# Sink column, merged weight sums, and value halves added in DRAM, in a one-core hybrid decoder layer

## Chip, cores and metric

The kernel runs on one core of a Trainium2 chip. The metric is the device time of one execution in microseconds; three timed runs of the kernel before gave 1900.37, 1901.0 and 1901.44 us, the median being 1901.0.

## What is computed

One layer of a hybrid decoder on x of 2048 tokens and 1024 channels, all in float32. After an RMS norm one input projection gives nine column groups. Branch A is a gated causal convolution of width 3. Branch B is sliding-window attention (window 128, 16 query heads, 4 key heads of 64, a norm on queries and keys, and a learned sink for every query head). Both branches are gated, projected, merged by sigmoid gates and projected once more.

```python
q = rms_norm(q.reshape(b, s, N_Q_HEADS, HEAD_DIM), q_norm_g)
k = rms_norm(k.reshape(b, s, N_KV_HEADS, HEAD_DIM), k_norm_g)
...
scores = einsum(qb, kb) * HEAD_DIM ** -0.5       # blocks of 128 queries, 256 keys
scores = where(valid, scores, NEG_INF)           # 0 <= q_pos - k_pos < 128
m = maximum(max(scores), sink)
p = exp(scores - m)
p = p / (sum(p) + exp(sink - m))
o = einsum(p, vb) * silu(z_a)
...
merged = g_a * (y_c @ w_conv_out) + g_b * (o @ w_attn_out)
return x + merged @ w_out
```

## The kernel before

**Tiles and products.** The sequence is cut into two tiles of 1024 tokens, which run one after the other. The projections are computed by a Strassen-like scheme: a unit of 256 output columns takes seven products (X, V, Y and so on) in place of eight, each product being twelve matmuls of 512 columns (`product`, L634: four chunks, and for each one high x high, high x low and low x high parts of the float32 numbers). Such a scheme needs sums of weight blocks and of input blocks. The sums of the weights are formed by VectorE in `sums` inside `pieces_of` (L516): one addition and three subtractions of 128x512 for a unit (two of the 81 units form them in another order, L528 and L535). ScalarE and VectorE then split each block into its high and low part.

**The clock of the program.** All order is written out by hand: `manual_schedule` keeps the order of issue on every engine. `run` (L889) advances a counter, the tick, with each product, and after each product issues what `put` has filed under that tick: pieces of weight preparation, evacuations and attention steps. Each engine has one queue and takes its instructions in that order; ScalarE, SyncE and GpSimd also issue transfers (SyncE most of them). `vec` (L284) weaves waiting VectorE steps in between others.

**Attention.** There are 64 blocks, 32 for each tile: 4 key heads by 8 blocks of 128 queries. `attention` (L1865) gives block r a tick n from the lists STEPS_0 and STEPS_1, three to nine ticks apart, and files its steps relative to n:

- n-5: loads of queries and keys (SyncE); n+4: load of values.
- n: `att_scores` (L1227). TensorE writes scores of both halves of the block and four heads into one score bank `s` (`sp`, one buffer): for each half one matmul of 384 columns (low parts of the keys), then two of 192 columns. VectorE copies the masked part over, takes the maximum (128 columns for each head), multiplies it with the query norm `rq`, takes the minimum with the negated sink, and adds the sink: five small results in `st`.
- n+1: `att_exp` (L1260). ScalarE takes the exponential of the sink term, and of the four heads with their sums.
- n+2: `att_norm` (L1270) adds the sink term, takes the reciprocal and scales; `att_flip` transposes 32x32 blocks on VectorE, and GpSimd stores the result `fd`; n+4: GpSimd loads it back transposed in four transfers.
- n+9 and n+10: ScalarE and VectorE form high and low parts (`xh`, `xl`); GpSimd masks them with four selects (`att_low`, L1303).
- n+13: `att_values` (L1324): six matmuls of 256 columns into a bank `po`.
- n+14: `att_out` (L1335). In `po` the partitions 0 to 63 and 64 to 127 hold two partial sums of the same result. ScalarE copies, crosswise, the other half of the partitions into `o`, with two copies of 64x256.
- n+15: `att_sum` (L1346). VectorE adds the own halves with two additions of 64x256, and SyncE stores `o` (128 KB) to `od` in DRAM.

The gate `za` loads `od` later (`fin_z`, L1422), in the order of the key heads, and multiplies it. Of the buffers, `big` has 19 slots of 2 KB a partition, which nearly all of the above share; `small` has 12 for each kind of small result.

Of the kernel before, what the change touches and what calls it, by code (L numbers as in the profile page):

```python
# [83 lines left out]
SUM_WAIT = 5  # L84
VALUES_LATER = ((0, 10), (0, 30))
# [40 lines left out]
def block_kernel(  # L126
# [23 lines left out]
    small = ctx.enter_context(tc.tile_pool(name="small", bufs=12))  # L150
# [68 lines left out]
    nsink_r = consts.tile([P, NKV, 2, 2], F32, name="nsink_r")  # L219
# [8 lines left out]
    def prep_cols():  # L228
# [5 lines left out]
        nc.vector.tensor_scalar(  # L234
            out=nsink_r, in0=sink_r, scalar1=-1.0, scalar2=None, op0=ALU.mult)
# [224 lines left out]
    def pieces_of(n):  # L460
# [37 lines left out]
        if kind in "SP":  # L498
# [509 lines left out]
    rqs = {}  # L1008
# [14 lines left out]
    def fin_q(t, j):  # L1023
# [58 lines left out]
        def by_query(r):  # L1082

            rq = consts.tile([P, 2, HB, 2, 2], F32, tag="rq", bufs=4, name=f"rq{t}_{j}")
            if not by_pe:
                vec.tensor_copy(rq, r.rearrange("p (c q b h) -> p q b h c", c=2, q=2, h=2))
                rqs[t, j] = rq
# [5 lines left out]
            rqs[t, j] = rq  # L1093
# [133 lines left out]
    def att_scores(t, j, b, ld):  # L1227
# [4 lines left out]
        sp = ps_s.tile([P, 2, 2, 2 * P], F32, tag="s", name=f"s{nm}")  # L1232
        for h in range(2):
            skip = (2 - h) * HD if first else 0
            keys = slice(h * HD + skip, (h + 3) * HD)
            nc.tensor.matmul(
                sp[:, h, :, skip : 3 * HD], lhsT=kq[:, 1, h * P : (h + 1) * P], rhs=kz[:, :, keys],
                start=True, stop=False)
            for c in range(2):
                nc.tensor.matmul(  # L1240
                    sp[:, h, c, skip : 3 * HD], lhsT=q2[:, h, c, :], rhs=kq[:, 0, keys],
                    start=False, stop=c == 1)
# [10 lines left out]
        mul(st[:, 5].rearrange("p (h c) -> p h c", c=2), st[:, 0].rearrange("p (h c) -> p h c", c=2), rv)  # L1253
        vec.scalar_tensor_tensor(
            out=st[:, 1], in0=st[:, 5], scalar=-1.0, in1=nsink_r[:, j].rearrange("p h c -> p (h c)"),
            op0=ALU.mult, op1=ALU.min)
        add(st[:, 2], sink_r[:, j].rearrange("p h c -> p (h c)"), st[:, 1])
        return sg, st, rv

    def att_exp(t, j, b, got):  # L1260
        sg, st, rv = got
        nc.scalar.activation(out=st[:, 3], in_=st[:, 2], func=AF.Exp)
        p = slot([P, G, P], F32, f"p{t}_{j}_{b}")
        for i in range(G):
            nc.scalar.activation(  # L1265
                out=p[:, i, :], in_=sg[:, i, HD : 3 * HD], func=AF.Exp, bias=st[:, 1, i : i + 1],
# [79 lines left out]
    def att_sum(t, j, b, got):  # L1346
        o, parts = got
        for ov, pv in parts:
            add(ov, pv, ov)
# [789 lines left out]
```

## Time and profile before

| what | value |
|---|---|
| median of three runs | 1901.0 us |
| profiled execution, its own time | 1900.13 us |
| its span, first to last instruction | 1898.4 us |
| TensorE matmul rows busy | 1888.9 us |
| VectorE busy | 1547.3 us |
| ScalarE busy | 986.6 us |
| GpSimd busy | 590.5 us |
| moved by DMA | 402.22 MB |

In the profile PE is TensorE's matmuls, PEld its weight loads, DVE VectorE, ACT ScalarE, POOL GpSimd and SP SyncE. Times are in microseconds, those of single instructions in nanoseconds. A group's row gives line, engine, operation, result and operands by the program's names, shapes, count, then busy time and mean; behind the second bar stands the idle time of the engine just before, and what ended it. A row of waits gives who waited for whom, the sum, how often, and the longest. Line 278 is that of a helper through which most VectorE steps go, so these are told apart by tile names. Matmuls overlap, so their durations are longer than the distance from one start to the next; the distance is what counts. Granted clock 1.00 is TensorE at full clock.

### The profile page before, as it was taken

To read this page: it belongs to the slowest core of one execution; us is meant where nothing else is said; L and a number is where in the kernel's file an instruction comes from. 1 tells how busy PE (TensorE), PEld (TensorE's weight loads), DVE (VectorE), ACT (ScalarE), POOL (GpSimd) and SP (SyncE) were. 2 spreads that over 40 slices of the span, in tenths; PEclk is the share of its full clock that TensorE was granted. 3 is DMA by queue.
4 is the path that set the end of the run, shared out by engine and by line. 5 is a ranking of instruction groups with operands and counts; after the bars stand their busy time and mean duration, and the time that the engine had idled before them with its cause. 6 is when DMAs were issued, how large, how long until landed. Compare 5 with 4: busy or idle time off the path is not lost.

```text
span 1898.4 us, 27426 instructions
## 1 busy us (share of the span) xinstructions
PE 1888.9 (100%) x8670; PEld 1572.3 (83%) x8670; DVE 1547.3 (82%) x2620; ACT 986.6 (52%) x1967; POOL 590.5 (31%) x846
## 2 busy tenths in 40 slices
PE   9999999999999999999999999999999999999999
PEld 7888888888888888888888888888888888888887
DVE  7988898898888767669799899888888777787754
ACT  7665455456666443434565545556666434444321
POOL 2073335335655000011462344445556000121000
PEclk9999999999999999999999999999999999999999
DMA  8286555558777857894584655567788887779653
GB/s 294 80 239 178 166 159 171 172 183 248 240 237 230 301 195 247 281 279 113 170 229 118 193 165 152 168 200 234 235 247 270 300 280 267 274 193 269 212 176 111
DMA packets 222497, 402.22 MB, mean 212 GB/s; under 512 B 30032, under 2 KB 104784, under 8 KB 212880
## 3 DMA queue, kind: packets, MB, share of 16 engines
q1 hardware_dynamic: 188224, 313.10, 50.4%
q0 software_dynamic: 30528, 78.94, 16.0%
q10 hardware_dynamic: 3600, 8.42, 1.3%
q8 instruction: 69, 1.13, 0.2%
q14 instruction: 76, 0.62, 0.1%
HBM read 271.09 MB, written 129.25 MB: 211 GB/s over the span
## 4 chain that ended last, share of the span: by engine, by line
PE 89%; DVE 5%; DMA 2%; ACT 2%; issue 1%; SPq 0%; POOL 0%; DVEq 0%; ACTq 0%; POOLq 0%
PE Y L640 33%; PE Xcv L640 4%; PE Vcv L640 4%; PE ya L1468 4%; PE Vq L640 2%; PE Xq L640 2%; PE Xyb L640 2%; PE Vyb L640 2%; PE Vo L640 2%; PE Xo L640 2%; PE Vza L640 2%; PE Xza L640 2%; PE po L1330 2%; PE Xgb L640 2%; PE Vgb L640 2%; PE Xga L640 2%
## 5 line engine op out<-in xcount | busy, mean ns | idle before, releaser
L1292 POOL DMA_DIRECT2D x<-fd x256 | 139.6, 552 | 128.8 <-DMA fd<-f 55.6
L1265 ACT ACTIVATE p<-s,st,rq 128x128 f32<-128x128 f32 x256 | 113.0, 450 | 0.1
L1313 POOL TENSOR_SCALAR_AFFINE_SELECT xh<-xh 64x512 fp32r<-64x512 f32 x64 | 59.3, 927 | 152.7 <-DVE xl L278 103.7
L1285 POOL DMA_DIRECT2D fd<-f x64 | 36.9, 577 | 209.4 <-DVE f L278 173.4
L1551 POOL DMA_DIRECT2D mt<-tha x16 | 13.8, 862 | 255.0 <-DVE tha L278 233.4
L640 PE MATMUL Xcv<-oph,wcv_ah 128*128 128x512 f32 x256 | 79.2, 390 | 0.0
L1313 POOL TENSOR_SCALAR_AFFINE_SELECT xl<-xl 64x512 fp32r<-64x512 f32 x64 | 66.2, 1034 | 4.4
L1313 POOL TENSOR_SCALAR_AFFINE_SELECT yp<-xl 64x512 fp32r<-64x512 f32 x64 | 58.2, 909 | 3.1
L1313 POOL TENSOR_SCALAR_AFFINE_SELECT yp<-yp 64x512 fp32r<-64x512 f32 x64 | 57.4, 898 | 4.2
L278 DVE SCALAR_TENSOR_TENSOR y<-u,cols,y 128x512 f32<-128x512 f32 x64 | 53.3, 834 | 3.8 <-ACT y L1379 2.7
L278 DVE TENSOR_TENSOR o<-po,o 64x256 f32<-64x256 f32 x128 | 53.4, 417 | 2.7 <-ACT o L1342 1.7
L640 PEld LDWEIGHTS Xcv<-oph,wcv_ah 128*128 128x128 f32 x256 | 47.6, 188 | 9.6
L278 DVE TENSOR_TENSOR p<-p,st 128x512 f32<-128x512 f32 x64 | 50.5, 790 | 3.3
L469 ACT CAST wcv_sh<-wcv_raw 128x1024 fp32r<-128x1024 f32 x16 | 16.8, 1051 | 69.7 <-DVE wcv_raw L278 69.7
L1265 ACT ACTIVATION_READ_ACCUMULATOR p<-s,st,rq 128x1 f32 x256 | 50.7, 198 | 0.0
L1342 ACT COPY o<-po 64x256 f32<-64x256 f32 x128 | 47.1, 368 | 6.2 <-DMA wpd_yb<-wph_yb 3.0
L1070 POOL DMA_DIRECT2D q2d<-q_h x64 | 44.2, 690 | 18.1 <-ACT q_h L1065 9.2
L640 PE MATMUL Xcv<-oph,wcv_al 128*128 128x512 f32 x128 | 49.8, 389 | 0.0
L2040 POOL DMA_DIRECT2D oc<-ocd x12 | 6.5, 543 | 136.0 <-DMA wyb_sh<-wpd_yb 119.7
L1070 POOL DMA_DIRECT2D q2d<-q_l x64 | 44.1, 689 | 13.7 <-DMA q2d<-q_h 5.0
L278 DVE TENSOR_TENSOR wcv_raw<-wcv_raw 128x512 f32<-128x512 f32 x64 | 47.3, 758 | 1.1
L278 DVE STREAM_TRANSPOSE f<-p 128x512 f32<-128x512 f32 x64 | 45.5, 711 | 2.9 <-DVE p L278 0.2
(713 smaller groups left out, 6457.9 us busy)
## 6 DMA issues: line engine op xcount, KB each, us to landing
gd<-th SPq DMA_DIRECT2D x64, 256.0 KB, 2.7
wcv_raw<-in_w_units SPq DMA_DIRECT2D x16, 1024.0 KB, 5.4
q<-q2d SPq DMA_DIRECT2D x64, 256.0 KB, 5.4
v<-vd SPq DMA_DIRECT2D x128, 128.0 KB, 3.5
fd<-f POOLq DMA_DIRECT2D x64, 256.0 KB, 4.4
x<-fd POOLq DMA_DIRECT2D x256, 64.0 KB, 3.2
th<-gd SPq DMA_DIRECT2D x48, 256.0 KB, 4.9
wga_raw<-in_w_units SPq DMA_DIRECT2D x8, 1024.0 KB, 5.3
```

Source lines behind the costliest of these rows:

```text
L278: r = f(*args, **kw)
L469: return (lambda: nc.scalar.copy(hi, src), lambda: vec.tensor_tensor(out=lo, in0=src, in1=hi.bitcast(F32), op=ALU.subtract))
L640: nc.tensor.matmul(ps, lhsT=w[:, j, :], rhs=b[:, m, :], start=start and j == 0 and i == 0, stop=j == KP - 1 and i == 2, skip_group_check=n ...
L1070: nc.gpsimd.dma_start(q2d[t][j][half, q * 2 * HB : (q + 1) * 2 * HB, i, e, :], src[HALVES[e]].bitcast(F32).rearrange("p (b x) -> p b x", x ...
L1265: nc.scalar.activation(out=p[:, i, :], in_=sg[:, i, HD : 3 * HD], func=AF.Exp, bias=st[:, 1, i : i + 1], scale=rv[:, i // 2, i % 2 : i % 2 ...
L1285: nc.gpsimd.dma_start(fd, f)
L1292: nc.gpsimd.dma_start(x[QUADS[k]], src[k])
L1313: nc.gpsimd.affine_select(out=d4, in_=s4, pattern=[[0, 2], [-32 * sg, 2], [0, G], [-sg, 32]], compare_op=ALU.is_gt if prev else ALU.is_ge, ...
L1330: nc.tensor.matmul(po[:, cs], lhsT=v2[:, kind + h, :], rhs=xx[:, :, h * HD : (h + 1) * HD], start=n == h == 0, stop=n == 2 and h == 1)
L1342: nc.scalar.copy(ov, pov[oth, :, e])
L1468: nc.tensor.matmul(ps, lhsT=w[:, j, cs], rhs=o[:, m, :], start=n == 0 and i == 0, stop=n == KC - 1 and i == 2)
L1551: nc.gpsimd.dma_start(mt[t][k, :, hs(q)], m, accum_op=ALU.add)
```

## The change

**Sink column.** For each query head's result `rq`, two new small VectorE steps compute the sink divided by it (`keep_query`). A new step `att_bank` at tick n-2 lets ScalarE copy the four sink values of a block into column 192 of the score bank. The maximum and the exponentials then run over 129 columns in place of 128, so the sink takes part in both, and the separate steps for it go: in `att_scores` two small VectorE steps and the negated sinks, in `att_exp` one small exponential, in `att_norm` one addition. The score matmuls change their order within each half: the two of 192 columns first, the one of 384 last.

**Merged weight sums.** The last two subtractions of a unit's sums become one of 128x1024, with the subtrahend read twice.

**Halves added in DRAM.** `att_out` copies `po` whole, with two copies of 128x256. VectorE's additions go. `att_store` stores partitions 0 to 63 from SyncE at tick n+15, and partitions 64 to 127 at n+17 from GpSimd to the same place in `od`, as an accumulating transfer. It must come after the first one has landed.

**Buffers.** `small` goes from 12 to 10 for each kind, `st` gets 4 of its own, and the slots of `big` grow by 16 bytes a partition.

```diff
-    small = ctx.enter_context(tc.tile_pool(name="small", bufs=12))
+    small = ctx.enter_context(tc.tile_pool(name="small", bufs=10))
...
                     summed.append(vec.chain(
-                        lambda: sub(raw[:, 1, 1], raw[:, 1, 1], raw[:, 0, 0]),
-                        lambda: sub(raw[:, 1, 0], raw[:, 1, 0], raw[:, 0, 0])))
+                        lambda: sub(raw[:, 1].rearrange("p h j c -> p h (j c)"),
+                                    raw[:, 1].rearrange("p h j c -> p h (j c)"),
+                                    raw[:, 0, 0].rearrange("p j c -> p (j c)").unsqueeze(1).to_broadcast(
+                                        [P, 2, H]))))
...
+    def keep_query(t, j, rq):
+        rqs[t, j] = rq
+        sr = sinks_of[t, j] = consts.tile(
+            [P, 2, HB, 2, 2], F32, tag="sr_", bufs=4, name=f"sinks{t}_{j}")
+        s4 = sr.rearrange("p q b h c -> p (q b) (h c)")
+        vec.reciprocal(out=s4, in_=rq.rearrange("p q b h c -> p (q b) (h c)"))
+        mul(s4, s4, sink_r[:, j].rearrange("p h c -> p (h c)").unsqueeze(1).to_broadcast([P, NB, G]))
...
+    def att_bank(t, j, b):
+        sp = ps_s.tile([P, 2, 2, 2 * P], F32, tag="s", name=f"s{t}_{j}_{b}")
+        nc.scalar.copy(sp[:, :, :, 3 * HD : 3 * HD + 1], sinks_of[t, j][:, b // HB, b % HB].unsqueeze(3))
+        return sp
...
-            nc.tensor.matmul(
-                sp[:, h, :, skip : 3 * HD], lhsT=kq[:, 1, h * P : (h + 1) * P], rhs=kz[:, :, keys],
-                start=True, stop=False)
             for c in range(2):
                 nc.tensor.matmul(
                     sp[:, h, c, skip : 3 * HD], lhsT=q2[:, h, c, :], rhs=kq[:, 0, keys],
-                    start=False, stop=c == 1)
+                    start=c == 0, stop=False)
+            nc.tensor.matmul(
+                sp[:, h, :, skip : 3 * HD], lhsT=kq[:, 1, h * P : (h + 1) * P], rhs=kz[:, :, keys],
+                start=False, stop=True)
...
-        st = small.tile([P, 6, G], F32, tag="st", name=f"st{nm}")
-        vec.tensor_reduce(out=st[:, 0], in_=sg[:, :, HD : 3 * HD], axis=AX.X, op=ALU.max)
-        mul(st[:, 5]..., st[:, 0]..., rv)
+        st = small.tile([P, 3, G], F32, tag="st", bufs=4, name=f"st{nm}")
+        vec.tensor_reduce(out=st[:, 0], in_=sg[:, :, HD : 3 * HD + 1], axis=AX.X, op=ALU.max)
         vec.scalar_tensor_tensor(
-            out=st[:, 1], in0=st[:, 5], scalar=-1.0, in1=nsink_r[:, j].rearrange("p h c -> p (h c)"),
-            op0=ALU.mult, op1=ALU.min)
-        add(st[:, 2], sink_r[:, j].rearrange("p h c -> p (h c)"), st[:, 1])
+            out=st[:, 1], in0=st[:, 0], scalar=-1.0, in1=rv.rearrange("p h c -> p (h c)"),
+            op0=ALU.mult, op1=ALU.mult)
...
-        nc.scalar.activation(out=st[:, 3], in_=st[:, 2], func=AF.Exp)
-        p = slot([P, G, P], F32, f"p{t}_{j}_{b}")
+        p = slot([P, G, P + 1], F32, f"p{t}_{j}_{b}")
...
-        o = slot([P, 2, P], F32, f"o{t}_{j}_{b}")
+        o = slot([P, 2, 2, P], F32, f"o{t}_{j}_{b}")
         for e in range(2):
-            own, oth = HALVES[e], HALVES[1 - e]
-            ov = o[own].rearrange("p c (h s q) -> p h s c q", h=2, s=2)
-            nc.scalar.copy(ov, pov[oth, :, e])
+            nc.scalar.copy(o[:, :, e].rearrange("p c (h s q) -> p h s c q", h=2, s=2), pov[:, :, e])
...
-        for ov, pv in parts:
-            add(ov, pv, ov)
+    def att_store(t, j, b, o, l):
+        to = od[t][2 * j : 2 * j + 2, :, b * P : (b + 1) * P].rearrange("c (e d) q -> d (c e) q", e=2)
+        src = o[HALVES[l]].rearrange("d c e q -> d (c e) q")
+        if l:
+            nc.gpsimd.dma_start(to, src, accum_op=ALU.add)
+        else:
+            nc.sync.dma_start(to, src)
...
+            put(n - 2, step("k", lambda g, j=j, b=b: att_bank(t, j, b)))
...
+            put(n + late + S_, step("t", lambda g, j=j, b=b: att_store(t, j, b, g["z"], 0)))
+            put(n + late + S_ + LOW_AT, step("u", lambda g, j=j, b=b: att_store(t, j, b, g["z"], 1)))
```

(`LOW_AT` is 2.)

More of the change, by code (lines that the diff above doesn't have):

```diff
@@ L1261, in att_exp @@
         sg, st, rv = got
-        nc.scalar.activation(out=st[:, 3], in_=st[:, 2], func=AF.Exp)
-        p = slot([P, G, P], F32, f"p{t}_{j}_{b}")
+        p = slot([P, G, P + 1], F32, f"p{t}_{j}_{b}")
         for i in range(G):
             nc.scalar.activation(
-                out=p[:, i, :], in_=sg[:, i, HD : 3 * HD], func=AF.Exp, bias=st[:, 1, i : i + 1],
-                scale=rv[:, i // 2, i % 2 : i % 2 + 1], accum_out=st[:, 4, i : i + 1])
-        return p, st
+                out=p[:, i, :], in_=sg[:, i, HD : 3 * HD + 1], func=AF.Exp, bias=st[:, 1, i : i + 1],
+                scale=rv[:, i // 2, i % 2 : i % 2 + 1], accum_out=st[:, 2, i : i + 1])
+        return p[:, :, 0:P], st
     def att_norm(got):
         p, st = got
-        add(st[:, 5], st[:, 4], st[:, 3])
-        vec.reciprocal(out=st[:, 0], in_=st[:, 5])
+        vec.reciprocal(out=st[:, 0], in_=st[:, 2])
         mul(p, p, st[:, 0].unsqueeze(2).to_broadcast([P, G, P]))
```

25 lines of the change are left out of this document (7 added, 18 removed).

## The prediction, made before the result was known

> **What bounds the kernel now.** I read the page's totals and its chain first, then a table of stretches, then the waits of TensorE, and then TensorE's own rows in time.
>
> ```profile
> span 1898.4 us, 27426 instructions
> PE 1888.9 (100%) x8670; PEld 1572.3 (83%) x8670; DVE 1547.3 (82%) x2620; ACT 986.6 (52%) x1967; POOL 590.5 (31%) x846
> PE 89%; DVE 5%; DMA 2%; ACT 2%; issue 1%; SPq 0%; POOL 0%; DVEq 0%; ACTq 0%; POOLq 0%
> ```
>
> The profiled execution took 1900.13 us, 1.7 more than its span; the median of the three timed runs, 1901.0, is 0.9 above it. TensorE is busy for all but 9.5 us of the span. A busy row can hide waiting, so the next table cuts the span into the stretches in which the attention blocks run (the first and the third row) and the one between them. Columns: stretch, its length, then busy us of PE, PEld, DVE, ACT and POOL, granted clock, DMA share, GB/s.
>
> ```profile
> 180.00:640.00 460.00, 459.74 (x2190) 386.11 (x2189) 401.08 (x695) 273.24 (x626) 207.68 (x288) 1.00 0.66 205
> 640.00:1030.00 390.00, 389.89 (x1732) 322.49 (x1731) 304.94 (x550) 182.37 (x304) 76.87 (x112) 1.00 0.71 216
> 1030.00:1490.00 460.00, 458.29 (x2179) 384.78 (x2178) 400.47 (x676) 264.63 (x614) 209.00 (x288) 1.00 0.66 205
> ```
>
> In the two attention stretches, where nearly everything that the diff touches runs, TensorE lacks 0.26 and 1.71 us, together 2.0. VectorE is busy for 87% of them. The waits of TensorE alone say the same:
>
> ```profile
> PE Y L1690 <- DVE zero L197: 1.5, 1, 1.5
> PE po L1330 <- POOL xl L1313: 0.9, 1, 0.9
> PE Y L640 <- DVE Vb L278: 0.4, 1, 0.4
> ```
>
> One of the 64 blocks made TensorE wait for GpSimd's masking. So work taken off VectorE can win at most those 2.0 us. Anything larger has to come from TensorE's own stream, and the chain in order of time shows where that stream is not at its best pace:
>
> ```profile
> 153.73 2.72 PE Y L640 x12
> 325.66 2.75 PE Vb L640 x12
> 331.90 2.81 PE Xb L640 x12
> ```
>
> A product of twelve 512-column matmuls takes 2.72 us undisturbed, 2.75 as the first one behind a value group (`po`), and 2.81 as the first one behind a score group (`s`). The score group itself, in the timeline:
>
> ```profile
> 330.97 0.33 PE L1236 MATMUL s<-lows,kq 128*128 128x384 f32 x1
> 331.14 0.36 PE L1240 MATMUL s<-kq,q 128*128 128x192 f32 x2
> 331.34 0.36 PE L1236 MATMUL s<-lows,kq 128*128 128x384 f32 x1
> 331.53 0.36 PE L1240 MATMUL s<-kq,q 128*128 128x192 f32 x2
> 331.73 0.66 PE L640 MATMUL Xb<-oph,wb_ah 128*128 128x512 f32 x2
> ```
>
> From start to start: 0.17 for the first wide matmul, 0.20 for two narrow ones, 0.19 for the second wide one (it follows narrow ones), 0.20: 0.76 us, and then a product that is 0.09 too long.
>
> **The change part by part.** *Order of the score matmuls.* Each half now runs narrow, narrow, wide in place of wide, narrow, narrow. No matmul is added or removed. From the starts above, both wide ones now follow narrow ones: 0.20 + 0.19 + 0.20 + 0.19 = 0.78, that is +0.02 a block. The next product then follows a wide matmul. No row shows that; the nearest one is the product behind `po`, which ends in 256 columns: 2.75. So a block changes by +0.02 − 0.06 = −0.04, and 64 blocks by −2.6 us, all of it on TensorE. Bounds: if the whole 0.09 goes, −0.07 × 64 = −4.5; if none goes, +0.02 × 64 = +1.3. I take −2.6, as the `po` row is the nearest.
>
> A rule that speaks against this term: the Trainium skill, page "TensorE: Matmul & The Clock Gate", sections "Back-to-back issue gap" and "LDWEIGHTS (loading the stationary operand)", has the spacing set by matmul and weight load together, with about N/2.4 + 2.5 ns for a warm matmul of N columns and P/1.2 ns for a load of P columns. By it a score group takes 4 × 107 + 2 × 162 = 0.75 us in either order (an estimate from that page), and the order is worth nothing. The trace's 0.76 agrees with that total; the 2.81 us product behind it is not in the rule.
>
> *VectorE.*
>
> ```profile
> L278 DVE TENSOR_TENSOR o<-po,o 64x256 f32<-64x256 f32 x128 | 53.4, 417 | 2.7 <-ACT o L1342 1.7
> L278 DVE TENSOR_TENSOR st<-cols,st 128x4 f32<-128x4 f32 x64 | 17.9, 280 | 2.2
> L278 DVE TENSOR_TENSOR st<-st,rq 128x4 f32<-128x4 f32 x64 | 15.9, 248 | 2.1
> L278 DVE TENSOR_TENSOR st<-st 128x4 f32<-128x4 f32 x64 | 13.6, 212 | 15.7 <-ACT p L1265 15.2
> L278 DVE TENSOR_TENSOR wcv_raw<-wcv_raw 128x512 f32<-128x512 f32 x64 | 47.3, 758 | 1.1
> L278 DVE TENSOR_TENSOR wcv_tl<-wcv_raw,wcv_th 128x1024 fp32r<-128x1024 f32 x16 | 19.4, 1214 | 0.1
> ```
>
> The first four groups go: 53.4 + 17.9 + 15.9 + 13.6 = 100.8 us. Merging two 128x512 subtractions into one of 128x1024 saves 2 × 0.758 − 1.214 = 0.30 us for each of 79 weight units (81 units form sums by the code, two of them in another order): 23.9. Added: a reciprocal and a product of 128x32 for each of 8 query heads' results, 16 small instructions at about 0.2 us (the small `st` rows), 3.2. Net −121 us, 8% of VectorE's busy time. VectorE isn't the bound, so the worth is what TensorE lacked, 0 to −2.0 us. I take half, −1.0: parts of that idle time are waits for ScalarE and GpSimd that only partly stem from VectorE. The merged subtraction blocks VectorE for 1.2 us in one piece; that is covered by the same slack.
>
> *ScalarE.*
>
> ```profile
> L1342 ACT COPY o<-po 64x256 f32<-64x256 f32 x128 | 47.1, 368 | 6.2 <-DMA wpd_yb<-wph_yb 3.0 <-DMA fd<-f 0.9
> L1262 ACT ACTIVATE st<-st 128x4 f32<-128x4 f32 x64 | 13.2, 205 | 50.3 <-DVE st L278 49.6
> 500.90 0.45 ACT L1265 ACTIVATE p<-s,st,rq 128x128 f32<-128x128 f32 x1
> 501.24 0.20 ACT L1265 ACTIVATION_READ_ACCUMULATOR p<-s,st,rq 128x1 f32 x1
> 502.11 0.22 PE L1236 MATMUL s<-lows,kq 128*128 128x128 f32 x1
> ```
>
> The two value copies keep 256 elements to the partition and grow from 64 to 128 partitions: no change. The small exponential (205 ns) goes, and a copy of four sink values into the score bank comes, about as long. The copy stands between the exponentials of one block and the score matmuls of the next, which share one bank. In one of the tightest places of the trace the exponentials end at 501.44 and the next scores start at 502.11: 0.67 us, which holds 0.2. Without the small exponential and two VectorE steps ahead of it, that moment also comes earlier. Cost 0; without that cover up to 0.2 us for each such block. One more column for the exponentials and for the maximum is nothing beside 450 ns.
>
> *The accumulating store.*
>
> ```profile
> L1551 POOL DMA_DIRECT2D mt<-tha x16 | 13.8, 862 | 255.0 <-DVE tha L278 233.4 <-DVE hr_r L305 9.7 <-DMA tha<-gd 4.6
> L1070 POOL DMA_DIRECT2D q2d<-q_h x64 | 44.2, 690 | 18.1 <-ACT q_h L1065 9.2 <-issue 2.3 <-DMA q2d<-q_h 1.7
> POOL xh L1313 <- DVE xl L278: 103.7, 32, 8.0
> od<-o SPq DMA_DIRECT2D x64, 128.0 KB, 2.5
> mt<-tha POOLq DMA_DIRECT2D x16, 256.0 KB, 5.4
> SPq L1350 <- DVE o L278: 118.6, 36, 13.6
> L1350 SPq DMA_DIRECT2D od<-o x64: 370/377/959, 227.3 to 1484.7; - x64
> L1428 SPq DMA_DIRECT2D zain<-od x32: 319/432/1532, 636.7 to 1565.1; - x32
> DMA packets 222497, 402.22 MB, mean 212 GB/s; under 512 B 30032, under 2 KB 104784, under 8 KB 212880
> ```
>
> GpSimd gets 64 issues. The kernel's own accumulating store costs 0.86 us to issue, a 64-partition store 0.69: 44 to 55 us, from 31% to 34% busy. Two things are queued behind such an issue: the masking of a later block, for which `po` waits, and the transposing DMAs. In 32 blocks GpSimd stands idle ahead of the masking for 3.2 us on average (103.7 / 32), waiting for VectorE's `xl`; 0.86 fits in there. The issue must also wait until SyncE's store of the other half has landed: 2.5 us after its issue, and two ticks, 5.4 us, lie between the two steps. SyncE's store itself comes earlier, since the 118.6 us that it spent waiting for VectorE's sum are gone. The block that already waits 0.9 us for the masking may get a full issue ahead of it: I take +0.9 for new waits in all, with 0 as the lower end and the first rival as the upper. The gate's loads of `od` have time: the last block of a tile belongs to the last key head, whose loads come last, in the second tile 80 us behind the last store. DMA volume grows by 64 × 128 KB written and read once more, 17 MB on 402, where DMA engines are busy two thirds of the time: 0. The slot of a result is held two ticks and a slower landing longer; no wait for such a slot shows now: 0.
>
> **Sum.** −2.6 − 1.0 + 0.9 = −2.7 us: the profiled execution would go from 1900.1 to 1897.4, and the median from 1901.0 to 1898.3.
>
> **The rivals.** *GpSimd becomes late (slower).* Two ticks are 5.4 us, but a store landing can take longer:
>
> ```profile
> DMA to landing us min/median/max: 1.8/2.5/9.6
> ```
>
> With a landing of 9.6 us, or when SyncE issues late because it waits for a weight buffer, GpSimd stands 4 us at its queue's head with the next masking behind it. TensorE loses what exceeds the slack of the values, say 1 us. It decides from about four such blocks on, which eat the gain; at ten blocks the time is 1901.0 − 3.6 + 10 = 1907. For it: the queue is in order and the wait is new. Against: the 118.6 us that SyncE is early now, and the 3.2 us of idle time. Chance 0.12.
>
> *The order is worth nothing.* If the 0.09 us come from the number of short matmuls and not from which is last, the term falls out: −1.0 + 0.9 = −0.1, 1900.9. For it: the product behind `po` is long too, without any narrow pair. Against: it is a third as long. It is also what the page's rule above would give. Chance 0.28.
>
> *Everything goes.* If the product behind a wide matmul is at 2.72, and all 2.0 us of idle time vanish: −4.5 − 2.0 = −6.5, 1894.5. For it: VectorE's relief of 8% falls mostly into the attention stretches. Against: some of that idle time has other causes. Chance 0.20.
>
> **How the numbers follow.** The forecast has the remaining 0.40. What a measurement can tell from no change here is about 0.2%, 3.8 us: below 1897.2 counts as faster, above 1904.8 as slower. The forecast's own spread (−1.3 to −4.2) puts a third of it, 0.13, beyond 1897.2; with "everything goes" faster is 0.33. Same: 0.27 + 0.28 = 0.55. Slower: 0.12. The range leaves out the slow rival and a little of the fast one: 1894.0 to 1902.5.
>
> **What would show it.** Right: the product behind a score group at about 2.75 us in the chain; the group at 0.78; VectorE near 1426 us busy; GpSimd near 640 us with 64 new issues of 0.7 to 0.9; no wait of TensorE for the score bank or the masking above 1 us. Wrong: products behind score groups still at 2.81; a row of GpSimd waiting for the store of `od` with several us a time, and `po` waiting for `xl` in many blocks; ScalarE or VectorE waiting for the slot of a result; TensorE busy well under 458 us in either attention stretch.

## The result and the profile after

The changed kernel takes 1918.41 us (median of five runs, 1914.91 to 1922.82), the kernel before 1901.14 beside it (five runs, 1900.37 to 1901.79). The ratio is 1.0091, with a 95% interval of 1.0080 to 1.0102: slower by 17 us, where the prediction had 1898.3 us and a range up to 1902.5. The profiled execution took 1918.41 us itself. A trace is of one execution, and executions of one kernel lie some us apart, so a trace's total can be off the median.

The page's totals after, and its chain:

```profile
span 1916.7 us, 27200 instructions
PE 1895.4 (99%) x8670; PEld 1576.3 (82%) x8670; DVE 1449.8 (76%) x2236; ACT 975.6 (51%) x1967; POOL 680.0 (35%) x910
PE 65%; DMA 2%; DVE 1%; POOL 1%; issue 1%; ACT 0%; SPq 0%; POOLq 0%; DVEq 0%; ACTq 0%
```

VectorE lost 97.5 us of work, 23 less than forecast, and GpSimd gained 89.5 where 44 to 55 were forecast (68.5 of busy time are the 64 new issues). TensorE now lacks 21 us of the span (9.5 before), and the rows that carry the chain are only 65% TensorE's. The stretches (the same as before) show where it lacks them:

```profile
180.00:640.00 460.00, 453.01 (x2150) 379.75 (x2148) 346.14 (x504) 261.71 (x615) 251.94 (x319) 1.00 0.73 207
640.00:1030.00 390.00, 388.43 (x1721) 320.11 (x1720) 303.74 (x529) 181.87 (x302) 77.92 (x113) 1.00 0.72 220
1030.00:1490.00 460.00, 453.05 (x2141) 380.67 (x2140) 344.92 (x505) 257.63 (x612) 246.02 (x314) 0.99 0.71 205
```

In each attention stretch TensorE lacks 7 us, in place of 0.3 and 1.7. The DMA share there has grown from 0.66 to 0.73 and 0.71. TensorE's waits:

```profile
PE po L1339 <- POOL xl L1322: 3.7, 4, 1.3
PE po L1339 <- POOL yp L1322: 3.6, 3, 1.5
PE s L1250 <- ACT s L1238: 3.3, 2, 2.5
PE Y L640 <- DVE Vz L276: 2.3, 1, 2.3
PE Y L640 <- ACT Y L658: 1.5, 1, 1.5
```

The value groups (`po`) wait for GpSimd's masking, the scores (`s`) for ScalarE's copy of the sinks, one product for VectorE and one for ScalarE.

**Where the 18 us lie.** Every trace has the same 8670 matmuls in the same order, but for the six of a score group. So the start of the n-th one can be subtracted between two traces, and the difference grows only where time is lost. It grows at five places. Times in the heading are those of the kernel before; the numbers are us lost against its profiled execution (1900.13 us). The last lines are kernels of the experiments below.

| kernel | 383 | 574 | 618-652 | 1354 | 1444-1484 | rest | total |
|---|---|---|---|---|---|---|---|
| changed kernel | 4.4 | 4.4 | 3.3 | 2.8 | 7.8 | -4.4 | 18.3 |
| without the sum in DRAM | 2.3 | 5.2 | 0.7 | 0.9 | 0.2 | -2.8 | 6.5 |
| the same, one load moved | 1.9 | -0.4 | 0.7 | 0.0 | 0.1 | -4.1 | -1.8 |
| sink column alone | 0.0 | 6.8 | -0.1 | 0.0 | 0.2 | -4.3 | 2.6 |
| sum in DRAM alone | 0.0 | 0.6 | 2.3 | 0.0 | 6.8 | 3.4 | 13.1 |

The gains that were forecast are there, in the column "rest"; five single places eat them. (In the last kernel "rest" holds a sixth place, 3.4 us lost near 480 us.)

Two things must be kept in mind with this table. Part of the losses is TensorE's clock: behind some of the waits the granted clock falls to 0.50 for 3.4 or 6.8 us (the last section shows one such place, worth 1.6 us). The changed kernel has three such stretches of 3.4 us, at 388, 1463 and 1477 us, so some 5 of its 18 us; the next one has one, the third none, the sink column alone 6.8 us near 576, the sum in DRAM alone one near 481 and one near 1471, and the kernel before none. And an entry of one trace is not firm: two kernels below, order_alone and order_behind, issue everything in the same order, and their traces lose 4.4 and 0.0 us at 383.

**The score group** went as forecast, but for its size. One group and the product behind it, after:

```profile
330.26 0.36 PE L1250 MATMUL s<-kq,q 128*128 128x192 f32 x2
330.46 0.36 PE L1253 MATMUL s<-lows,kq 128*128 128x384 f32 x1
330.66 0.36 PE L1250 MATMUL s<-kq,q 128*128 128x192 f32 x2
330.85 0.36 PE L1253 MATMUL s<-lows,kq 128*128 128x384 f32 x1
331.05 0.63 PE L640 MATMUL Xb<-oph,wb_ah 128*128 128x512 f32 x2
...
333.80 0.62 PE L640 MATMUL Y<-oph,wb_th 128*128 128x512 f32 x2
```

The group takes 331.05 - 330.26 = 0.79 us and the product behind it 2.75 (0.76 and 2.81 before; 0.78 and 2.75 forecast). Over the 64 blocks the medians are +0.029 and -0.062.

**The places near 1447 us.** SyncE, GpSimd and TensorE there, after:

```profile
1447.03 0.38 SPq L438 DMA_DIRECT2D wz_raw<-in_w_units  x1
1447.50 0.62 SPq L1357 DMA_DIRECT2D od<-o  x1
1448.18 1.87 SPq L1596 DMA_DIRECT2D wos<-in_w_out  x2
```

```profile
1449.54 0.58 POOL L1294 DMA_DIRECT2D fd<-f  x1
1458.36 1.06 POOL L1355 DMA_DIRECT2D od<-o  x1 [8.24 <-DMA od<-o]
1459.04 1.15 POOL L1322 TENSOR_SCALAR_AFFINE_SELECT xh<-xh 64x512 fp32r<-64x512 f32 x1
1460.24 0.74 POOL L1322 TENSOR_SCALAR_AFFINE_SELECT yp<-yp 64x512 fp32r<-64x512 f32 x1
```

```profile
1461.82 0.50 PE L1339 MATMUL po<-yp,v 128*128 128x256 f32 x2 [1.08 <-POOL yp L1322]
1462.97 0.51 PE L1339 MATMUL po<-xl,v 128*128 128x256 f32 x2 [0.65 <-POOL xl L1322]
1463.31 4.50 PE L640 MATMUL Y<-oph,wz_d 128*128 128x512 f32 x12
```

SyncE issues the store of the first half directly behind a weight load of 1 MB. The store lands 10.1 us later. GpSimd stands 8.24 us at the head of its queue, with the masking behind it, and the value group waits twice. This is the first rival's mechanism, step by step. The product that follows takes 4.50 us in place of 2.72, most of it at half the clock. The next value group, near 1476 us, waits 1.55 and 1.19 us for another reason: GpSimd's masking stood 4.91 us for VectorE's `xl`, and that for the landing of a store of `f`:

```profile
1470.84 0.69 DVE L276 TENSOR_TENSOR xl<-x,xh 128x512 fp32r<-128x512 f32 x1 [3.84 <-DMA fd<-f]
```

**The place near 1354 us** shows another way to lose time, a slot. ScalarE, then TensorE:

```profile
1365.17 0.65 ACT L1348 COPY o<-po 128x256 f32<-128x256 f32 x2 [7.28 <-DMA od<-o]
1365.71 0.18 ACT L1238 COPY s<-sinks 128x4 f32<-128x4 f32 x1
```

```profile
1365.94 0.47 PE L1250 MATMUL s<-kq,q 128*128 128x192 f32 x2 [2.49 <-ACT s L1238]
```

ScalarE's copy of `po` waits 7.28 us for a slot that an earlier result holds until its accumulating store, issued at 1355.7 us, has landed, 9.5 us later. The copy of the sinks stands behind it on ScalarE, and the scores wait 2.49 us for that.

### The profile page after: what moved, and what is told of

It reads as the page before. It is cut to its first block, busy times and chain, and to the rows that moved or that the text cites. A ratio compares the mean times of both kernels' runs of the same rounds, so it can differ in the third digit from the quotient of the medians.

```text
span 1916.7 us, 27200 instructions
## 1 busy us (share of the span) xinstructions
PE 1895.4 (99%) x8670; PEld 1576.3 (82%) x8670; DVE 1449.8 (76%) x2236; ACT 975.6 (51%) x1967; POOL 680.0 (35%) x910
## 2 busy tenths in 40 slices
DMA packets 239902, 410.58 MB, mean 214 GB/s; under 512 B 31056, under 2 KB 122192, under 8 KB 230288
## 4 chain that ended last, share of the span: by engine, by line
PE 65%; DMA 2%; DVE 1%; POOL 1%; issue 1%; ACT 0%; SPq 0%; POOLq 0%; DVEq 0%; ACTq 0%
PE Y L640 24%; PE ya L1474 4%; PE Vcv L640 2%; PE Xcv L640 2%; PE Xyb L640 2%; PE Vo L640 2%; PE Xo L640 2%; PE Vyb L640 2%; PE Vza L640 2%; PE Xza L640 2%; PE Xz L640 1%; PE Vz L640 1%; DMA od<-o 1%; PE po L1339 1%; PE Vga L640 1%; PE Vb L640 1%
## 5 line engine op out<-in xcount | busy, mean ns | idle before, releaser
L1275 ACT ACTIVATE p<-s,st,rq 128x129 f32<-128x129 f32 x256 | 114.4, 461 | 34.8 <-DVE st L276 25.6
L1322 POOL TENSOR_SCALAR_AFFINE_SELECT xh<-xh 64x512 fp32r<-64x512 f32 x64 | 66.4, 1038 | 103.2 <-DVE xl L276 65.9
L1355 POOL DMA_DIRECT2D od<-o x64 | 68.5, 1070 | 91.2 <-DMA od<-o 64.9
L1322 POOL TENSOR_SCALAR_AFFINE_SELECT xl<-xl 64x512 fp32r<-64x512 f32 x64 | 71.8, 1123 | 4.4
L1322 POOL TENSOR_SCALAR_AFFINE_SELECT yp<-xl 64x512 fp32r<-64x512 f32 x64 | 72.0, 1125 | 3.1
L276 DVE TENSOR_TENSOR xl<-x,xh 128x512 fp32r<-128x512 f32 x64 | 43.9, 686 | 20.5 <-issue 6.7
L1250 PEld LDWEIGHTS s<-kq,q 128*128 128x128 f32 x256 | 46.1, 189 | 7.8 <-ACT s L1238 3.9
L1308 ACT CAST xh<-x 128x512 fp32r<-128x512 f32 x64 | 40.0, 625 | 19.2 <-PE po L1339 6.5
```

The lines of the kernel that those rows point to most:

```text
L276: r = f(*args, **kw)
L1250: nc.tensor.matmul(sp[:, h, c, skip : 3 * HD], lhsT=q2[:, h, c, :], rhs=kq[:, 0, keys], start=c == 0, stop=False)
L1275: nc.scalar.activation(out=p[:, i, :], in_=sg[:, i, HD : 3 * HD + 1], func=AF.Exp, bias=st[:, 1, i : i + 1], scale=rv[:, i // 2, i % 2 : i ...
L1308: nc.scalar.copy(xh, pt)
L1322: nc.gpsimd.affine_select(out=d4, in_=s4, pattern=[[0, 2], [-32 * sg, 2], [0, G], [-sg, 32]], compare_op=ALU.is_gt if prev else ALU.is_ge, ...
L1355: nc.gpsimd.dma_start(to, src, accum_op=ALU.add)
```

## The experiments

The theory after the result: the accumulating store waits at the head of GpSimd's queue, and the masking comes late. Rivals: the issue's own time on GpSimd, the DMA traffic, the copy of the sinks. The kernel before took 1900.7 to 1901.2 us (median) beside every experiment; ratios are against it.

**no_dram_sum**: `att_out` and `att_sum` of the kernel before put back.

```diff
-            put(n + late + S_, step("t", ... att_store(t, j, b, g["z"], 0)))
-            put(n + late + S_ + LOW_AT, step("u", ... att_store(t, j, b, g["z"], 1)))
+            put(n + late + S_, step("t", ... att_sum(t, j, b, g["z"])))
```

> The changed kernel with the addition of the value halves put back on VectorE and the store of the result on SyncE alone, as before; the sink column, the order of the score matmuls and the merged weight sums stay. Theory (the accumulating store stands at the head of GpSimd's queue until the other half has landed, and the masking behind it comes late): nearly all of the loss goes, 1897 to 1899 us, GpSimd near 600 us busy, no wait of TensorE for the masking above 1.5 us. Rival A (part of the loss comes from the copy of the sinks into the score bank, which TensorE waits for): 1902 us or more, with rows of TensorE waiting for that copy.

Measured: 1906.5 us, ratio 1.0026 (1.0016 to 1.0036). A third of the loss stays without the sum in DRAM; the theory is not the whole, and rival A's 1902 or more comes true without its reason: the wait for the copy of the sinks isn't among the rows. The largest is another:

```profile
PE Y L639 <- DVE Vz L275: 4.3, 2, 3.9
PE po L1338 <- POOL xl L1321: 1.9, 2, 1.4
```

**dram_sum_alone**: the kernel before with the new `att_out` and `att_store` only.

> The kernel before with the addition in DRAM alone: no sink column, the old order of the score matmuls, single weight sums. Theory: the loss is all here, 1916 to 1922 us (17 us, and the 2.6 us that the order of the score matmuls no longer gives back). Rival A: at most 1910 us, since the wait for the bank copy is absent.

Measured: 1912.4 us, 1.0061 (1.0047 to 1.0075). Two thirds of the loss; the expected 1916 was too high, and rival A's 1910 too low. 11.7 here and 5.8 in the kernel above add up to the changed kernel's 17.

**plain_elsewhere** and **plain_same_place**: the store of the second half without its addition.

```diff
-            nc.gpsimd.dma_start(to, src, accum_op=ALU.add)
+            nc.gpsimd.dma_start(to, src)      # plain_same_place; plain_elsewhere: to another tensor
```

> The changed kernel, where GpSimd's store of the second half is a plain one to another tensor in DRAM: the sum of the halves is left out. It has the issue on GpSimd and the bytes, but nothing to wait for except its data. Theory (the wait): 1898 to 1902 us, and GpSimd's wait for the landing of the other store (64.9 us) is gone. Rival B (the cost of 64 issues of about 1 us on GpSimd): 1910 us or more. Rival C (the DMA traffic): 1905 us or more.

> The changed kernel, where GpSimd's store of the second half goes to the same place as the first but overwrites it in place of adding: the sum of the halves is left out. GpSimd still waits until the first half has landed. Theory (the wait): 1910 to 1917 us, close to the changed kernel's 1918. Rival D (the accumulation itself, through its slow landing and its traffic in DRAM): 1900 to 1904 us.

Measured: 1908.2 us, 1.0039 (1.0025 to 1.0053), and 1910.0, 1.0050 (1.0035 to 1.0066). Set against the 1906.5 of the kernel without the sum in DRAM, issue and bytes cost 1.7 and the wait for the first half 1.8, each within the error. Adding in place of overwriting costs 8.4 more, with a like wait for the first half (64.9 us on GpSimd, 52.1 with the plain store). The theory for the first kernel (1898 to 1902) missed. That for the second (1910 to 1917) holds only at its lower end, and rival D (1900 to 1904) had not counted what the kernel loses without any store. The queues of the two kernels that write the same bytes to the same place, plain first:

```profile
q0 software_dynamic: 33600, 87.33, 17.1%
```

```profile
q0 software_dynamic: 47936, 87.33, 19.5%
```

Before, this queue had 30528 packets. A plain store makes (33600 - 30528) / 64 = 48, an accumulating one 272. GpSimd's issue takes 1.07 us in place of 0.63, and the median landing 5.5 us in place of 4.6.

**What costs 5 us near 574 us.** In the traces with the sink column TensorE loses 4.4 to 8.0 us there, half clock included (2.2 in the kernel below with both stores on GpSimd, less where the load named below is moved behind the store), and without it at most 0.6. The rows of the kernel without the sum in DRAM, SyncE, GpSimd, VectorE and TensorE in turn:

```profile
569.24 0.33 SPq L437 DMA_DIRECT2D wz_raw<-in_w_units  x1
```

```profile
568.15 1.69 POOL L1321 TENSOR_SCALAR_AFFINE_SELECT xl<-xl 64x512 fp32r<-64x512 f32 x1
569.80 0.58 POOL L1293 DMA_DIRECT2D fd<-f  x1
```

```profile
568.00 1.21 DVE L275 TENSOR_TENSOR wz_tl<-wz_raw,wz_th 128x1024 fp32r<-128x1024 f32 x1
...
577.59 0.69 DVE L275 TENSOR_TENSOR xl<-x,xh 128x512 fp32r<-128x512 f32 x1 [7.61 <-issue]
```

```profile
580.79 1.22 PE L639 MATMUL Y<-oph,wz_th 128*128 128x512 f32 x2 [3.86 <-DVE Vz L275]
```

And the kernel before, GpSimd and SyncE:

```profile
565.30 0.76 POOL L1313 TENSOR_SCALAR_AFFINE_SELECT xl<-xl 64x512 fp32r<-64x512 f32 x1
566.02 0.58 POOL L1285 DMA_DIRECT2D fd<-f  x1
```

```profile
567.62 0.33 SPq L440 DMA_DIRECT2D wz_raw<-in_w_units  x1
```

Before, GpSimd's store of `f` goes out 1.6 us ahead of the weight load and lands after 4.6 us. Now the load goes first, by 0.56 us: it waits for VectorE's last reading of the old weights (`wz_tl`), which, counted from VectorE's step `wz_sl`, comes 1.0 us earlier, mostly by the three small steps a block that the sink column removed; and the store comes 1.15 us later, as GpSimd's selects take longer in all, the last one, beside that VectorE step, 1.69 us in place of 0.76. The store lands after 7.7 us, at 577.5. By the order in which the program hands out its slots, VectorE's `xl` is to be written into the slot of just that `f`: VectorE stands for 7.61 us ("issue" in the row; the landing falls on its end), and everything behind it with it.

**load_behind**: the kernel without the sum in DRAM, where SyncE issues this one load at the end of its tick.

```diff
-            ahead_loads()
+            if tick[0] not in BEHIND:          # BEHIND = (186,)
+                ahead_loads()
...
+            if tick[0] in BEHIND:
+                ahead_loads()
```

> The changed kernel without the sum in DRAM (the 1906.5 us kernel), in which one weight load, that of the unit z2 at tick 186, is put behind the other steps of its tick on SyncE's queue, so that it is issued after GpSimd's store of f and not before it. Nothing else differs. Theory (the load of 1 MB overtakes the store, the store lands late, VectorE waits for its slot and TensorE for VectorE): the 5.4 us at the product near 574 us go, 1900.5 to 1902.5 us, and VectorE no longer stands idle for 7.6 us ahead of xl. Rival (VectorE's wait has another cause, such as instruction fetch or the sink copies): still 1905 to 1908 us.

Measured: 1898.6 us, 0.9990 (0.9981 to 0.9999): 8 us faster than the kernel without this edit (5.6 of it at this place, by the two traces), 2 us faster than before, and the fastest kernel of this study.

```profile
568.01 0.58 POOL L1297 DMA_DIRECT2D fd<-f  x1
```

```profile
569.91 0.56 SPq L438 DMA_DIRECT2D wz_raw<-in_w_units  x1
```

```profile
571.16 0.69 DVE L276 TENSOR_TENSOR xl<-x,xh 128x512 fp32r<-128x512 f32 x1 [2.96 <-ACT s5z L667]
```

With the store ahead it lands in 3.1 us, and the loss at 574 is gone (-0.4 in the table). So this cause is shown.

**order_alone**, **sink_alone**, **sums_alone**: one part of the change each on the kernel before (the sink column brings the order with it).

> The kernel before with nothing but the new order of the score matmuls (two narrow ones, then the wide one, in each half). Theory, from the rows of the changed kernel (0.797 us from start to start in a group in place of 0.766, but 0.012 too much in the product behind it in place of 0.083): 40 ns a block, 64 blocks, 2.6 us less, 1898 to 1899 us beside 1900.7 to 1901.1. Rival (the order is worth nothing on its own): 1900.5 to 1901.5.

> The kernel before with the sink column (and with it the new order of the score matmuls) and the smaller pools; weight sums and the sum of the halves as before. Theory (a faster VectorE frees the weight buffer earlier; the next weight load of 1 MB then goes ahead of GpSimd's store of f near 570 us, whose landing VectorE waits for with TensorE behind it): if the sink part alone is enough for that, 1903 to 1907 us with 4 to 5 us lost at the product near 574 us; if not, 1898 to 1900. Rival (the copy of the sinks into the score bank holds up the scores): 1902 us or more with waits of the scores for that copy.

> The kernel before with nothing but the merged weight sums. Theory: VectorE frees the weight buffers up to 0.3 us earlier a unit; if that alone makes the load overtake the store of f, 1905 to 1907 us; if not, 1900.5 to 1901.5. Rival (one piece of 1.2 us on VectorE hurts GpSimd's masking, which runs slower beside it): losses at the value groups, 1903 us or more with waits of TensorE for the masking.

Measured: 1903.1 us, 1.0009 (1.0000 to 1.0018); 1901.6, 1.0006 (0.9997 to 1.0015); 1900.6, 1.0001 (0.9992 to 1.0010). The merged sums are worth nothing that can be measured. The sink column alone is enough for the collision: its trace loses 6.8 at 574 and gains 4.3 elsewhere; its median still lies below the 1903 to 1907 expected for that case. The order alone missed both of its ranges. Its eleven runs spread from 1898.87 to 1905.19 us, and the trace is of the slowest: the score groups with their products gain 1.1 us in all (26 ns a block at the median), and 4.4 are lost at 383 us, where a store of `f`, issued behind a weight load at the same times as before, landed after 9.2 us in place of 5.5.

**after_behind**: the changed kernel with the same edit. **store_from_act**: first half stored by ScalarE's queue. **both_pool**: by GpSimd's. **later_4**: `LOW_AT = 4`.

```diff
-            nc.sync.dma_start(to, src)
+            nc.scalar.dma_start(to, src)       # store_from_act; both_pool: nc.gpsimd
...
-LOW_AT = 2
+LOW_AT = 4                                 # later_4
```

> The changed kernel as it is, sum in DRAM included, with the one weight load (unit z2, tick 186) put behind the other steps of its tick on SyncE's queue. Theory (two separate causes: this load that overtakes the store of f, worth 3.7 us in the changed kernel's trace, and the accumulating store, worth the rest): 1912 to 1915 us, and the losses at the value groups near 383, 1447 and 1457 us and at the scores near 1363 us stay. Rival (one cause: once the load is in order, the accumulating store fits into GpSimd's slack): 1899 to 1904 us.

> The changed kernel, where the first half of each result is stored from ScalarE's queue right behind its copies in place of from SyncE's. Theory (SyncE issues that store late, because it stands behind weight loads that wait for a buffer, and GpSimd waits for its landing): GpSimd's wait for the landing falls from 64.9 us to below 20 and the 7.4 us near 1447 and 1457 us go, 1908 to 1912 us. Rival (the accumulating issue of 1.07 us itself, and the slower landing): 1915 us or more.

> The changed kernel, where GpSimd stores both halves: the first at tick n+15 as a plain store, the second two ticks later as the accumulating one. Theory (the lateness of SyncE's store): GpSimd pays 64 more issues of 0.63 us, 40 us in all, but its wait for the landing falls to below 25 us; 1910 to 1915 us. Rival (GpSimd's own load: each issue pushes the masking): 1920 us or more.

> The changed kernel with the accumulating store four ticks after the first one in place of two. Theory (GpSimd waits at its queue's head for the landing): the wait of 64.9 us falls to below 25, 1909 to 1913 us. Rival (the slots, held 5 us longer by each result): ScalarE or VectorE waits for a slot, 1917 us or more.

Measured: 1919.2 us, 1.0095 (1.0081 to 1.0109); 1921.8, 1.0112 (1.0093 to 1.0132); 1940.1, 1.0205 (1.0191 to 1.0218); 1927.4, 1.0138 (1.0119 to 1.0157). None of the four hit its theory; the rivals of the last three gave the right times. In the first, GpSimd was later than in the kernel without the sum in DRAM, and the load, though moved, still went 0.2 us ahead of the store of `f` (572.41 and 572.60 us), so it decided nothing. The others speak against the wait as the sole cause: it fell from 64.9 us to 44.9 and to 38.0 in the second and the last, and both got slower. The last kernel's longest waits of TensorE, then two of GpSimd and VectorE:

```profile
PE Vz L640 <- ACT wz_sh L467: 9.4, 2, 5.2
PE s L1250 <- DMA q<-q2d: 4.7, 1, 4.7
```

```profile
POOL od L1355 <- DMA od<-o: 38.0, 4, 21.0
DVE xl L276 <- DMA od<-o: 10.4, 2, 9.2
```

Two ticks later GpSimd hardly waits in the attention stretches, but VectorE waits 10.4 us for slots that the results now hold longer. In the kernel with both stores on GpSimd its wait even grew, to 95.2 us.

**two_behind**, **order_behind**: the load of unit ga1 at tick 123 to be moved too, on the kernel of load_behind and on that of order_alone. **after_two_behind**: both loads on the changed kernel, z2 to the end of tick 187.

> The 1898.6 us kernel (no sum in DRAM, the load of z2 put back in its tick) with a second weight load put back in the same way: the unit ga1 at tick 123, behind which GpSimd's store of f near 371 us took 7.2 us to land. Theory (loads that go ahead of a store of f): the 1.9 us that are lost at the value group near 383 us go, 1896 to 1897.5 us. Rival (that loss is GpSimd's masking slowed beside VectorE): 1898 to 1899.5 us.

> The kernel before with the new order of the score matmuls and the load of ga1 put back to the end of tick 123. Theory (the order is worth 2.6 us, and the 4.4 us at 383 us in the run of the order alone came from a store of f that landed 9.2 us after its issue, behind that load): 1897.5 to 1899 us. Rival (the order alone costs something else): 1901 to 1903.5 us.

> The changed kernel as it is, sum in DRAM included, with both weight loads put back: ga1 to the end of tick 123, z2 to the end of tick 187 (in the run that put it back to the end of tick 186, the load was still issued 0.2 us ahead of the store of f). Theory (the load ahead of the store of f is a cause by itself in the changed kernel too): the losses near 383 us (4.4) and 574 us (3.7 to 4.8) go, 1909 to 1912 us, and those near 627, 1354, 1447 and 1457 us stay. Rival (the accumulating store alone makes GpSimd and the slots late): 1915 us or more.

Measured: 1899.8 us, 0.9992 (0.9983 to 1.0001); 1900.1, 0.9999 (0.9990 to 1.0008); 1916.0, 1.0075 (1.0062 to 1.0088). In the traces the edit of tick 123 moved nothing: SyncE issues everything in the same order as without it, and the load still goes ahead of the store of `f` (370.30 and 370.86 us in order_behind, 370.62 and 371.18 in order_alone; 368.48 and 369.85 in two_behind). So the third tests the load of z2 alone, and the first two are a second measurement each: 1898.6 and 1899.8 for the kernel of load_behind, 1903.1 and 1900.1 for the order alone, with intervals that overlap. The median of all 22 runs of the order alone is 1900.9, which can't be told from no change. Where the trace of order_alone lost 4.4 us at 383, that of order_behind has no loss, and the store of `f` landed after 6.5 us in place of 9.2: that loss comes and goes between executions, and the expectation that named this load as its cause wasn't tested. In the third the load of z2 goes 4.2 us behind the store of `f` (574.88 and 570.68 us), and its trace lost 1.9 at 574 in place of 4.4, but still 4.3 at 383, and more at 618 to 652 and 1354; it missed its 1909 to 1912. In the changed kernel this load is one cause among several, and what one fix frees, other waits take.

**plain_same_select**: a select of 64x256 on GpSimd ahead of each plain store. **accum_elsewhere**: the accumulating store to a place of its own, without a wait for the first half.

```diff
+            nc.gpsimd.affine_select(out=half, in_=half, pattern=[[0, 2 * P]], compare_op=ALU.is_ge, ...)
             nc.gpsimd.dma_start(to, src)                               # plain_same_select
...
-            nc.gpsimd.dma_start(to, src, accum_op=ALU.add)
+            nc.gpsimd.dma_start(there, src, accum_op=ALU.add)          # accum_elsewhere
```

> The 1910 us kernel (second half overwrites the first in place of adding to it, so the sum of the halves is left out) with one more select of 64x256 on GpSimd ahead of each such store, which leaves the data as they are: GpSimd is busy for about as long as with the accumulating store (0.4 us more a block), but the store lands as a plain one does. Theory (GpSimd's time is what the accumulation costs): 1916 to 1921 us. Rival (the accumulating store's later landing, 5.5 us in place of 4.6, which holds its slot longer): 1909 to 1912 us.

> The changed kernel, where GpSimd's accumulating store of the second half goes to one of four small places in DRAM that nothing else reads, in place of onto the first half: the sum of the halves is left out. The store accumulates, but needn't wait for the first half to land. Theory (the accumulating transfer itself, with 272 packets a store in place of 48 and a DMA share of 0.73 in place of 0.69, makes other transfers and its own slot late): 1914 to 1918 us, near the changed kernel's 1918. Rival (the wait for the first half is what costs): 1907 to 1910 us, as with the plain store to another place (1908.2).

Measured: 1909.9 us, 1.0049 (1.0035 to 1.0062): 37 us more work on GpSimd changed nothing, so its time isn't what adding costs. And 1912.9 us, 1.0060 (1.0048 to 1.0073), between the theory and the rival. Four kernels make a square:

| | no wait for the first half | wait |
|---|---|---|
| plain store | 1908.2 | 1910.0 |
| accumulating store | 1912.9 | 1918.4 |

The accumulating transfer costs 4.7 us without the wait and 8.4 with it, the wait 1.8 without accumulating and 5.5 with it. Only across the steps of 8.4 and 5.5 do the intervals of the ratios not overlap. So each of the two costs something where the other is present; that together they cost more than their sum (by 3.7 us) is within the error and not shown.

**dram_sum_first18**: the kernel of load_behind, with the sum in DRAM for the first 18 of the 32 blocks of a tile.

```diff
+            if r < 18:
+                put(... att_store(t, j, b, g["z"], 0)) ... att_store(t, j, b, g["z"], 1)
+            else:
+                put(... att_sum(t, j, b, g["z"]))
```

> The 1898.6 us kernel (sink column, order and merged sums, the load of z2 put back in its tick), with the sum in DRAM for the first 18 of the 32 blocks of each tile and VectorE's sum for the other 14. Theory (the transfers and the issue cost something only where blocks follow each other after three ticks, at the end of each tile, and near 383 us): 1898 to 1903 us. Rival (the extra traffic costs everywhere alike, 36 of the 64 blocks having it): 1907 to 1911 us.

Measured: 1901.6 us, 1.0002 (0.9993 to 1.0011), as the theory had it: with 36 of 64 blocks it is 2 to 3 us slower than the two measurements of load_behind's kernel, about as much as the error, and its trace loses 3.5 at 1354 us. With all 64 blocks and the load of z2 behind the store (after_two_behind) it is 1916.0. Most of what the sum in DRAM costs therefore comes with the other 28 blocks, which stand three to five ticks apart.

## Why the prediction was wrong

**The step that failed first** is the cost of the accumulating store: "The issue must also wait until SyncE's store of the other half has landed: 2.5 us after its issue, and two ticks, 5.4 us, lie between the two steps", with +0.9 us for new waits in all. Measured, the sum in DRAM costs 11.9 us (1906.5 to 1918.4). The 2.5 us were the median landing of the old store. The new first half lands after 3.9 us at the median and 10.7 at most, and GpSimd waits for it 15 times:

```profile
DMA to landing us min/median/max: 2.4/3.9/10.7
```

```profile
POOL od L1355 <- DMA od<-o: 64.9, 15, 19.2
```

The wait is not all of it. Only 8.8 of the 64.9 us lie in the first attention stretch and 36.9 in the second, and TensorE lacks 7 us in each. By itself, with a plain store, the wait is worth 1.8 us, within the error. The accumulating transfer, which had no term of its own, costs 4.7 us without the wait and 8.4 with it.

**Two terms costed at nothing** belong to it. "DMA volume grows by ... 17 MB on 402 ...: 0" was 8.4 MB by the page (402.22 before, 410.58 after), and counted bytes alone; a store makes 272 packets, and the DMA share went from 0.66 to 0.73. "The slot of a result is held two ticks and a slower landing longer; no wait for such a slot shows now: 0" took the waits of the kernel before for those of the new one; the 7.28 us on ScalarE and the run with later stores show that price.

**The first rival had the right sign**, and its steps are seen one by one near 1447 us. Its 1907 at ten blocks was too low, and its reason, the wait, is by itself only a part.

**VectorE's relief.** "VectorE isn't the bound, so the worth is what TensorE lacked, 0 to -2.0 us" had no lower side. The waits of the kernel before did shrink, but a VectorE that is done earlier lets the next weight load go earlier, ahead of a store that the kernel needs: +5.2 us at one place. No rival named that. Moving that load showed it, and with it moved, the rest of the change gives 1898.6 us (1899.8 in the second measurement), where the sum of the terms without the store would have been 1901.0 - 3.6 = 1897.4.

The relief itself was 97.5 us in place of 121: the prediction took one group's subtractions, 0.758 us each, for all units, where those of `wza`, `wo` and `wq` take 0.69 us, so the merged sums saved about 16 us in place of 23.9.

**The order** was right in both rows and too large: -0.062 + 0.029 us a block by medians, and 26 to 35 ns a block in the traces, 1.1 to 2.2 us in all, in place of 2.6. The forecast held in the rows; in the times, the order by itself can't be told from nothing. **ScalarE's bank copy** at 0 held: the scores wait for it twice, where ScalarE is itself late (2.49 us behind the wait for a slot, 0.80 us near 594), and not at all with the sink column alone. **The accumulating issue** took 1.07 us in place of 0.69 to 0.86; by the run with the extra select that time costs nothing that can be measured.

What stays open: by which way the accumulating transfer makes the others late (its packets, the traffic of reading and writing, or its own landing) wasn't separated, nor why the store of `f` issued near 371 us lands after 5.5 us in one run and 9.2 in another with the same issue times. What costs 4.2 to 4.4 us at 383 and 3 to 5 us at 618 to 652 in the changed kernel and in the two kernels that move its loads, wasn't followed to a cause. A 20th slot, which would test the price of slots by itself, wasn't tried.

## What to carry to other kernels

A step that moves from an engine into a transfer can be paid in landings: look up not only the median landing but the longest, and what is issued just ahead of it, and ask who waits for its slot. When an engine gets faster, look for what its release starts (here a weight load) and which smaller transfer that then overtakes. Subtracting the starts of the same matmul in two traces turns "1% slower" into a handful of places, each of which can be read in the timeline. A second trace of the same kernel tells which of them are firm, and the order of issue in the trace tells whether an edit moved what it was meant to move.

## What the runs showed of the hardware that was not expected

**A short stall halves the clock for a while.** Behind the two waits near 1462 us, 1.08 and 0.65 us, the product runs at the clock of this row of stretches:

```profile
1463.40:1467.20 3.80, 3.80 (x12) 2.93 (x11) 3.19 (x4) 2.69 (x4) 3.36 (x6) 0.56 0.62 131
```

The matmuls start 427 ns apart in place of 227, eight in a row, and each such episode costs 1.6 us on top of the stall; the changed kernel has three of them at value groups. The Trainium skill, page "TensorE: Matmul & The Clock Gate", section "Part 1: The HAM clock gate (the "warmup" mystery)", has the half clock after an idle window of about 3.4 us. The two states agree with these rows; the idle time doesn't, as less than 2 us of waiting were enough here. In the kernel of load_behind one wait of 1.37 us near 386 us was not enough: its clock stays at 1.00 from 380 to 390 us.

**GpSimd's selects beside VectorE.** The same select takes 0.76 us or 1.69, and the longer one began while VectorE's subtraction of two operands (568.00, 1.21 us) ran. The Trainium skill, page "SBUF — State Buffer", section "SBUF: two separate sides", says that a GpSimd operation and a VectorE operation with two inputs in SBUF lock each other out for a whole instruction; the rows roughly agree: 0.76 and the rest of VectorE's step, 1.06, make 1.82, where 1.69 was measured.

**An accumulating store is cut finer.** 128 KB make 272 packets as an accumulating store and 48 as a plain one to the same place, by the counts of the software queue above.
